# The modulation silu(c) @ ada_w in a hybrid decoder layer: float32 products on 32-column strips of TensorE in place of multiply-adds on VectorE

## The chip, the core and the metric

The kernel runs on one core of a Trainium2 chip. The core's engines each work through a queue of their own, in order: TensorE (PE: matrix products, and the loads of their weights), VectorE (DVE), ScalarE (ACT), GpSimd (POOL), and SyncE (SP), whose queue issues nearly all of the DMAs. SBUF is the working memory, PSUM the eight banks into which PE writes. The metric is the device time of one execution in microseconds, lower is better.

## What is computed

One decoder layer on x (1024 tokens x 1024 features, float32) with a conditioning vector c of 1024 numbers. Cut to what matters here:

```
mod = silu(c) @ ada_w + ada_b                  # ada_w: 1024 x 6144
sh1, sc1, g1, sh2, sc2, g2 = split(mod, 6)     # 1024 numbers each
h  = rmsnorm(x, norm1_g) * (1 + sc1) + sh1
q, k, v, u = split(h @ w_in, 4)                # 512 columns each
o  = [rmsnorm(stick_breaking(q, k, v)), rmsnorm(s5(u))]
x  = x + g1 * (o @ w_out)
h  = rmsnorm(x, norm2_g) * (1 + sc2) + sh2
val, gate = split(causal_dwconv(h @ ffn_w_up), 2)
x  = x + g2 * ((gelu(gate) * val) @ ffn_w_down)
```

The change concerns the first line alone: a vector times a matrix of 24 MB, all in float32.

## The kernel before

Big products are made of float32r parts: an operand is split into hi and lo, and hi*hi + hi*lo + lo*hi are accumulated in PSUM, three products of 128x512 each. Smaller ones are plain float32. The program is written in the order of the work; a scheduler then sets the order of the instructions on each engine's queue, and tile pools with a fixed number of buffers (`bufs`) decide how early a load or a product may begin.

**Stage 1 (about 11 to 103 us): modulation of norm1, h, and the columns u.** For each feature block k = 0..7, 1 MB of ada_w (`ada_raw`, three buffers) holds 8 row blocks r of 128 rows, with 128 shift and 128 scale columns. For k = 0 PE makes the products directly, with the weights as the stationary operand and one column of c moving (L210, sixteen products of 128x1). For k = 1..7 DVE multiplies and adds: one TENSOR_SCALAR (L213) and seven SCALAR_TENSOR_TENSOR (through the helper `stt`, L67) on 128x256 into `ada_acc`; then two PE products with a column of ones (L218) sum over the 128 partitions. DVE adds bias and gain (S1c, A1); ACT applies them to the transposed x (L233) and splits off hi, POOL makes lo, and PE accumulates u (`u_mm`, L190 to L192). On DVE's queue this work is mixed with the parameters of the state-space part (`st`, `ek`, `Q`).

**Stage 2 (about 103 to 344 us): q, k, v and the state-space groups.** PE makes 24 token tiles of 24 products (`qkvp`, L551 to L553); in between stand four batches of the state-space part, whose products (`w1p`, `kp`, `vps`, `yps`, `gps`, float32) alternate with DVE's scans. `ada_back` (six calls of 512 columns: two for g1, two for sh2, two for sc2) is spread over the token tiles, three steps ahead of each: a step loads one row block (`ada_raw`, 256 KB) and DVE adds it into `ada_acc` (L67, 128x512). After eight steps PE sums over the partitions (`adps`, L571 or L575). Loads and `ada_acc` share the three buffers of the tag `uF`. PSUM: `psA` has four buffers of the tag `aux`, three of `mm`, one of `qt`.

**Attention (344 to 610 us)** and the output projections are not touched. **The MLP (640 to 1365 us)** is 22 pairs of up-projection tiles (`upps`, L916 to L918) and down-projections (`dnps`). `g2_rows` stands after the first pair: 16 row blocks of ada_w are added by DVE (L968, L67) into `g2acc`, and PE sums over the partitions (L972).

Of the kernel before, what the change touches and what calls it, by code (L numbers as in the profile page):

```python
# [20 lines left out]
D = 1024  # L21
# [14 lines left out]
def hybrid_layer_kernel(  # L36
# [23 lines left out]
    def tt(eng, out, a, b, op):  # L60
        eng.tensor_tensor(out=out, in0=a, in1=b, op=op)  # L61
# [9 lines left out]
    def rsqrt(pl, dst, v, n):  # L71
        """dst = 1 / sqrt(v), [128, n], to float32's accuracy."""
# [13 lines left out]
    # packed small parameters, one column (or row, on each partition) after the other  # L86
# [3 lines left out]
    cols2_sb = const.tile([128, 194], F32, name="cols2_sb")  # L90
# [3 lines left out]
    gq_sb, gk_sb = cols2_sb[:, 192:193], cols2_sb[:, 193:194]  # L94

# [9 lines left out]
    # added to the scores of the block on the diagonal: -1e30 where key >= query  # L105
# [7 lines left out]

    u_d = dram.tile([512, 8, 128], F32, name="u_d")
# [5 lines left out]
    # modulation: per-feature scale and shift columns, per-feature gate rows  # L120
# [6 lines left out]
    # ================= phase A: norm1, input projection, state space groups =================  # L127
# [35 lines left out]
    # per-token scale of norm1  # L163
# [35 lines left out]
    for k in range(NK):  # L199
# [5 lines left out]
        # shift and scale of 128 features  # L205
        mps = psU.tile([128, 512], F32, tag="mps", name="mps", bufs=1)
        if k == 0:
            for i in range(2):
                for r in range(8):
                    pe.matmul(mps[:, i:i + 1], lhsT=raw[:, r, i * 128:(i + 1) * 128], rhs=c_sb[:, r:r + 1], start=(r == 0), stop=(r == 7))  # L210
        else:
            acc = pn.tile([128, 256], F32, tag="ada_acc", name="ada_acc1")
            dve.tensor_scalar(out=acc, in0=raw[:, 0, :], scalar1=c_sb[:, 0:1], scalar2=None, op0=MUL)  # L213
            for r in range(1, 8):
                stt(acc, raw[:, r, :], c_sb[:, r:r + 1], acc, MUL, ADD)
            for i in range(2):
                cs_ = slice(i * 128, (i + 1) * 128)
                pe.matmul(mps[:, i:i + 1], lhsT=acc[:, cs_], rhs=ones[:, 0:1], start=True, stop=True)  # L218
        tt(dve, S1c[:, k:k + 1], mps[:, 0:1], sh1b[:, k:k + 1], ADD)
        stt(A1[:, k:k + 1], mps[:, 1:2], sc1b[:, k:k + 1], n1g_sb[:, k:k + 1], ADD, MUL)  # L220
# [90 lines left out]
    # powers a^1..a^8: pw[:, ri, k, pair]  # L311
# [22 lines left out]
    def cmul(eng, ore, oim, are, aim, bre_, bim_, tmp, conj=False):  # L334
        """(ore + i oim) = (are + i aim) * (bre + i bim), or * conj(b)"""
# [30 lines left out]
    # conj(e^{i 8 theta})^(2^k), k = 0..6  # L366
# [6 lines left out]
    # b * (e^{dt a} - 1) / a, in place  # L373
# [12 lines left out]
    # e^{-i 8 theta c} for c = 0..15, and for c = 0, 16, .. 112  # L386
# [9 lines left out]
    # coefficients of a pair of groups side by side, each on the partitions of its own states  # L396
# [6 lines left out]
    # delta(p div 16, j)  # L403
    blkid = sm.tile([128, 8], F32, name="blkid")
    dve.tensor_reduce(out=blkid, in_=ident.rearrange("p (j h) -> p j h", h=16), op=ADD, axis=AX.X)
    # delta(p mod 16, h)
# [13 lines left out]
    psA = alloc("psA", bufs=4, space=PSUM)  # L420
# [6 lines left out]
    def ssm_batch(ft):  # L427
        q0 = ft * 4
        qs = slice(q0, q0 + 4)
        # rotation table e^{-i 8 theta c}  # L430
# [3 lines left out]
        # Q[(par, p), pair, i, h] = a^{7-i} b  # L434
# [10 lines left out]
        # coefficients of the state's real and imaginary part in Re(C a^{j+1} s)  # L445
# [7 lines left out]
        # inputs of the groups: partition = (step in chunk, channel), free = chunk  # L453
# [4 lines left out]
        # transposed Q for the products with the inputs  # L458
# [5 lines left out]
        # impulse response inside a chunk, block lower triangular  # L464
# [17 lines left out]
        # chunk sums, rotated, then scanned over the chunks  # L482
# [46 lines left out]
        for j in range(8):  # L529
            sp.dma_start(out=ov[j], in_=gt[j * 16:(j + 1) * 16])  # L530

# [1 line left out]
    def load_wchunk(cix):  # L533
        his, los = [], []
        for k in range(NK):
# [554 lines left out]
```

## Time and profile before

| | us |
|---|---|
| median of three runs | 1371.71 (1368.38 to 1372.44) |
| the profiled execution: span from its first to its last instruction | 1365.3 |
| PE busy | 1261.6 (92%) |
| DVE busy | 953.0 (70%) |
| ACT busy, POOL busy | 375.6 (28%), 385.3 (28%) |
| mean granted TensorE clock, as a share of full speed | 0.959 |

The profile is of one execution, whose own time is known by its span; what lies around the span is not in the profile. Busy time of PE is modelled for the ends of its products, so that products in a row overlap: their rate is read from the distance of their starts. TensorE's clock has two levels, 2.4 GHz (1.00 in the profile's column) and 1.2 GHz; a value between them is a mean over a stretch.

### The profile page before, as it was taken

The page shows a single profiled execution, that of the slowest core. Times are in us where ns is not written, and L with a number is a line of the kernel's source. Part 1 is how long each engine was busy: PE and PEld are TensorE (multiplying, and loading weights), DVE is VectorE, ACT ScalarE, POOL GpSimd, SP SyncE. Part 2 cuts the span into 40 slices and gives each one's busy share as a digit, 9 for nine tenths or more (in the row PEclk, how much of TensorE's full clock was granted, in tenths as well). Part 3 has the DMA queues.
Part 4 walks back from the last instruction along what each step waited for, and adds up shares of the span by engine and source line. Part 5 has one row for each costly group of instructions (what it writes and reads, how often), then busy time and mean ns, then how long its engine had stood idle before and what let it go on. Part 6 is the DMA issues. An engine that isn't in the chain of part 4 may idle for free.

```text
span 1365.3 us, 16015 instructions
## 1 busy us (share of the span) xinstructions
PE 1261.6 (92%) x5988; PEld 1034.5 (76%) x5988; DVE 953.0 (70%) x1465; ACT 375.6 (28%) x651; POOL 385.3 (28%) x369
## 2 busy tenths in 40 slices
PE   5979899898778996898999999999999999999998
PEld 4767778677557785676788888888888888888886
DVE  6999999873998889875775555455465655555555
ACT  5431233431765666444111101010101010101010
POOL 3562461530684449512130101111111111111100
PEclk9889889999889998898999999999999999999999
DMA  8452445657934663000620102020211111111103
GB/s 342 149 139 63 122 142 141 157 169 230 242 97 145 213 187 106 32 16 20 199 91 31 62 31 78 16 77 18 75 42 56 46 57 47 47 47 47 47 1 123
DMA packets 98264, 134.78 MB, mean 99 GB/s; under 512 B 33414, under 2 KB 66310, under 8 KB 97164
## 3 DMA queue, kind: packets, MB, share of 16 engines
q1 hardware_dynamic: 81292, 125.38, 29.5%
q10 hardware_dynamic: 16896, 8.39, 2.2%
q8 instruction: 47, 0.77, 0.2%
q14 instruction: 29, 0.24, 0.1%
HBM read 107.40 MB, written 25.17 MB: 97 GB/s over the span
## 4 chain that ended last, share of the span: by engine, by line
PE 64%; DVE 20%; DMA 7%; issue 3%; POOL 2%; ACT 2%; SPq 1%; DVEq 0%; ACTq 0%; POOLq 0%
PE upps L916 11%; PE upps L917 11%; PE upps L918 11%; PE dnps L1004 6%; PE dnps L1005 6%; PE dnps L1003 6%; DVE ada_acc L67 3%; DMA ada_raw<-in_ada_r_dram 3%; DVE nb L700 2%; PE wops L773 2%; PE wops L774 1%; PE wops L775 1%; POOL sig L61 1%; DVE st L61 1%; DMA x<-in_x_dram 1%
## 5 line engine op out<-in xcount | busy, mean ns | idle before, releaser
L916 PE MATMUL upps<-h2hi,uphi 128*128 128x512 f32 x704 | 275.5, 391 | 2.3 <-DVE cv L67 2.0
L917 PE MATMUL upps<-h2lo,uphi 128*128 128x512 f32 x704 | 274.6, 390 | 0.2 <-DVE h2lo L61 0.2
L918 PE MATMUL upps<-h2hi,uplo 128*128 128x512 f32 x704 | 274.4, 390 | 0.0
L953 ACT ACTIVATE cv<-upps,cols_sb 128x1024 f32<-128x1024 f32 x44 | 53.2, 1209 | 500.3 <-PE upps L918 500.3
L916 PEld LDWEIGHTS upps<-h2hi,uphi 128*128 128x128 f32 x704 | 132.4, 188 | 30.8 <-issue 2.8
L917 PEld LDWEIGHTS upps<-h2lo,uphi 128*128 128x128 f32 x704 | 132.4, 188 | 28.1 <-DVE h2lo L61 0.5
L918 PEld LDWEIGHTS upps<-h2hi,uplo 128*128 128x128 f32 x704 | 132.4, 188 | 27.6 <-issue 0.2
L61 DVE TENSOR_TENSOR uplo<-upraw,uphi 128x1024 fp32r<-128x1024 f32 x44 | 55.5, 1262 | 127.1 <-POOL uphi L161 127.1
L1004 PE MATMUL dnps<-wdlo,ahi 128*128 128x512 f32 x352 | 137.0, 389 | 0.9 <-DVE wdlo L61 0.9
L1003 PE MATMUL dnps<-wdhi,ahi 128*128 128x512 f32 x352 | 136.6, 389 | 0.6 <-POOL wdhi L161 0.6
L1005 PE MATMUL dnps<-wdhi,alo 128*128 128x512 f32 x352 | 136.9, 389 | 0.0
L161 POOL TENSOR_SCALAR uphi<-upraw 128x1024 fp32r<-128x1024 f32 x44 | 47.5, 1080 | 281.1 <-PE upps L917 200.0
L61 DVE TENSOR_TENSOR xs<-dnps,xs 128x512 f32<-128x512 f32 x88 | 60.9, 692 | 86.9 <-PE dnps L1005 86.9
L67 DVE SCALAR_TENSOR_TENSOR cv<-upps,cols_sb,cv 128x1023 f32<-128x1023 f32 x88 | 112.4, 1278 | 11.6 <-ACT cv L953 10.9
L61 POOL TENSOR_TENSOR sig<-sig,nb 128x127 f32<-128x127 f32 (+3 forms) x64 | 98.2, 1542 | 70.5 <-DVE nb L700 47.4
L700 DVE TENSOR_TENSOR_SCAN nb<-nb 128x128 f32<-128x128 f32 (+3 forms) x64 | 105.8, 1667 | 8.0 <-ACT nb L698 7.6
L67 DVE SCALAR_TENSOR_TENSOR ada_acc<-ada_raw,c_sb,ada_acc 128x256 f32<-128x256 f32 (+1 forms) x97 | 74.2, 779 | 24.5 <-DMA ada_raw<-in_ada_r_dram 21.2
L551 PE MATMUL qkvp<-w_hi,hhi 128*128 128x512 f32 x192 | 78.5, 410 | 3.4 <-DVE qssq L604 2.9
L552 PE MATMUL qkvp<-w_lo,hhi 128*128 128x512 f32 x192 | 78.5, 409 | 0.6 <-POOL w_lo L61 0.6
L553 PE MATMUL qkvp<-w_hi,hlo 128*128 128x512 f32 x192 | 78.0, 406 | 0.0
L1004 PEld LDWEIGHTS dnps<-wdlo,ahi 128*128 128x128 f32 x352 | 66.1, 188 | 15.0 <-DVE wdlo L61 1.3
L1003 PEld LDWEIGHTS dnps<-wdhi,ahi 128*128 128x128 f32 x352 | 65.9, 188 | 14.7 <-POOL wdhi L161 1.0
(240 smaller groups left out, 2370.7 us busy)
## 6 DMA issues: line engine op xcount, KB each, us to landing
upraw<-in_w_up_dram SPq DMA_DIRECT2D x44, 512.0 KB, 3.2
ada_raw<-in_ada_r_dram SPq DMA_DIRECT2D x48, 256.0 KB, 2.8
wdraw<-in_w_down_dram SPq DMA_DIRECT2D x22, 512.0 KB, 3.8
ada_raw<-in_ada_a_dram SPq DMA_DIRECT2D x8, 1024.0 KB, 9.3
qk_d<-hl ACTq DMA_DIRECT2D x32, 256.0 KB, 2.8
q<-qk_d SPq DMA_DIRECT2D x32, 256.0 KB, 5.7
w_raw<-in_w_qkv_dram SPq DMA_DIRECT2D x24, 256.0 KB, 3.9
xt<-in_x_dram SPq DMA_DIRECT2D x8, 512.0 KB, 5.5
```

The source lines that it names most:

```text
L61: eng.tensor_tensor(out=out, in0=a, in1=b, op=op)
L67: dve.scalar_tensor_tensor(out=out, in0=a, scalar=s, in1=b, op0=op0, op1=op1)
L551: pe.matmul(o, lhsT=lh, rhs=his[k], start=(k == 0), stop=False)
L552: pe.matmul(o, lhsT=lh, rhs=los[k], start=False, stop=False)
L553: pe.matmul(o, lhsT=ll, rhs=his[k], start=False, stop=(k == NK - 1))
L700: dve.tensor_tensor_scan(out=nb[:, 0:n][:, ::-1], data0=nb[:, 0:n][:, ::-1], data1=nb[:, 0:n][:, ::-1], initial=1.0, op0=MUL, op1=ALU.bypass)
L916: pe.matmul(o, lhsT=hi[:, k, :], rhs=rh, start=(k == 0), stop=False)
L917: pe.matmul(o, lhsT=hi[:, k, :], rhs=rl, start=False, stop=False)
L918: pe.matmul(o, lhsT=lo[:, k, :], rhs=rh, start=False, stop=(k == NK - 1))
L1003: pe.matmul(o, lhsT=hi[:, a], rhs=whi[:, b], start=(i == 0), stop=False)
L1004: pe.matmul(o, lhsT=hi[:, a], rhs=wlo[:, b], start=False, stop=False)
L1005: pe.matmul(o, lhsT=lo[:, a], rhs=whi[:, b], start=False, stop=(i == len(ops) - 1))
```

## The change

The vector silu(c) becomes the stationary operand. `c32` holds each row block's 128 values 32 times side by side, so that a product with `c32[:, r, :]` occupies 32 columns of the array and writes 32 equal rows of PSUM; row blocks r and r + 4 accumulate in strip r % 4, and the four strips fill the 128 partitions of one PSUM tile. That tile is copied to SBUF, and a product with a matrix of 1/32 (`mean32`) sums over the partitions. In stage 1 this serves all eight feature blocks, k = 0 too. In stage 2 the PSUM tile has a tag of its own (`ada`, one buffer), for which `aux` goes from four buffers to three; the accumulator in `uF` is needed only after the eighth row block. The biases of sh2 and sc2 come in `cols2` (16 more columns); that of g1 is loaded on all partitions.

```diff
-    cols2_sb = const.tile([128, 194], F32, name="cols2_sb")
+    cols2_sb = const.tile([128, 210], F32, name="cols2_sb")
...
+    sh2b, sc2b = cols2_sb[:, 194:202], cols2_sb[:, 202:210]
...
+    c32 = const.tile([128, 8, 32], F32, name="c32")
+    dve.tensor_copy(c32, c_sb.unsqueeze(2).to_broadcast([128, 8, 32]))
+
+    mean32 = const.tile([128, 128], F32, name="mean32")
+    pool.memset(mean32, 1.0 / 32.0)
+
+    def strips(ps, raws):
+        for r in range(8):
+            j = r % 4
+            pe.matmul(ps[32 * j:32 * j + 32], lhsT=c32[:, r, :], rhs=raws[r], start=(r < 4), stop=(r >= 4))
...
         mps = psU.tile([128, 512], F32, tag="mps", name="mps", bufs=1)
-        if k == 0:
-            for i in range(2):
-                for r in range(8):
-                    pe.matmul(mps[:, i:i + 1], lhsT=raw[:, r, i * 128:(i + 1) * 128], rhs=c_sb[:, r:r + 1], start=(r == 0), stop=(r == 7))
-        else:
-            acc = pn.tile([128, 256], F32, tag="ada_acc", name="ada_acc1")
-            dve.tensor_scalar(out=acc, in0=raw[:, 0, :], scalar1=c_sb[:, 0:1], scalar2=None, op0=MUL)
-            for r in range(1, 8):
-                stt(acc, raw[:, r, :], c_sb[:, r:r + 1], acc, MUL, ADD)
-            for i in range(2):
-                cs_ = slice(i * 128, (i + 1) * 128)
-                pe.matmul(mps[:, i:i + 1], lhsT=acc[:, cs_], rhs=ones[:, 0:1], start=True, stop=True)
-        tt(dve, S1c[:, k:k + 1], mps[:, 0:1], sh1b[:, k:k + 1], ADD)
-        stt(A1[:, k:k + 1], mps[:, 1:2], sc1b[:, k:k + 1], n1g_sb[:, k:k + 1], ADD, MUL)
+        strips(mps[:, 0:256], [raw[:, r, :] for r in range(8)])
+        acc = pn.tile([128, 256], F32, tag="ada_acc", name="ada_acc1")
+        dve.tensor_copy(acc, mps[:, 0:256])
+        for i in range(2):
+            pe.matmul(mps[:, 256 + i:257 + i], lhsT=acc[:, i * 128:(i + 1) * 128], rhs=mean32[:, 0:1], start=True, stop=True)
+        tt(dve, S1c[:, k:k + 1], mps[:, 256:257], sh1b[:, k:k + 1], ADD)
+        stt(A1[:, k:k + 1], mps[:, 257:258], sc1b[:, k:k + 1], n1g_sb[:, k:k + 1], ADD, MUL)
...
-    psA = alloc("psA", bufs=4, space=PSUM)
+    psA = alloc("psA", bufs=3, space=PSUM)
...
     def ada_back(ix):
         kind, o = divmod(ix * 512, 1024)
-        acc = wp.tile([128, 512], F32, tag="uF", name="ada_acc", bufs=3)
-        pool.memset(acc, 0.0)
-        sp.dma_start(out=acc[0:1, :], in_=ada_br[ix:ix + 1, :])
+        ps = psA.tile([128, 512], F32, tag="ada", name="adps", bufs=1)
+        if kind == 0:
+            sp.dma_start(out=g1row[:, o:o + 512], in_=ada_br[ix:ix + 1, :].to_broadcast([128, 512]))
         for r in range(8):
             raw = wp.tile([128, 512], F32, tag="uF", name="ada_raw", bufs=3)
             sp.dma_start(out=raw, in_=ada_r[ix, :, r])
-            stt(acc, raw, c_sb[:, r:r + 1], acc, MUL, ADD)
+            j = r % 4
+            pe.matmul(ps[32 * j:32 * j + 32], lhsT=c32[:, r, :], rhs=raw, start=(r < 4), stop=(r >= 4))
             yield
-        ps = psA.tile([128, 512], F32, tag="aux", name="adps")
+        acc = wp.tile([128, 512], F32, tag="uF", name="ada_acc", bufs=3)
+        act.activation(out=acc, in_=ps, func=AF.Copy)
         if kind == 0:
-            pe.matmul(ps, lhsT=ones, rhs=acc, start=True, stop=True)
-            act.activation(out=g1row[:, o:o + 512], in_=ps, func=AF.Copy)
+            pe.matmul(ps, lhsT=mean32, rhs=acc, start=True, stop=True)
+            tt(dve, g1row[:, o:o + 512], ps, g1row[:, o:o + 512], ADD)
         else:
             for j in range(4):
-                pe.matmul(ps[:, j:j + 1], lhsT=acc[:, j * 128:(j + 1) * 128], rhs=ones[:, 0:1], start=True, stop=True)
+                pe.matmul(ps[:, j:j + 1], lhsT=acc[:, j * 128:(j + 1) * 128], rhs=mean32[:, 0:1], start=True, stop=True)
...
     def g2_rows():
         for ix in range(6, 8):
...
+            ps = psD.tile([128, 512], F32, tag="dn", name="adps2", bufs=4)
+            for r in range(0, 8, 2):
+                raw = wq.tile([128, 2, 512], F32, tag="wdraw", name="g2raw", bufs=2)
+                sp.dma_start(out=raw, in_=ada_r[ix, :, r:r + 2])
+                for i in range(2):
+                    j = (r + i) % 4
+                    pe.matmul(ps[32 * j:32 * j + 32], lhsT=c32[:, r + i, :], rhs=raw[:, i, :], start=(r < 4), stop=(r >= 4))
             acc = wq.tile([128, 512], F32, tag="wdhi", name="g2acc", bufs=2)
-            for r in range(8):
-                if r % 2 == 0:
-                    raw = wq.tile([128, 2, 512], F32, tag="wdraw", name="g2raw", bufs=2)
-                    sp.dma_start(out=raw, in_=ada_r[ix, :, r:r + 2])
-                if r == 0:
-                    dve.tensor_scalar(out=acc, in0=raw[:, 0, :], scalar1=c_sb[:, 0:1], scalar2=None, op0=MUL)
-                else:
-                    stt(acc, raw[:, r % 2, :], c_sb[:, r:r + 1], acc, MUL, ADD)
-            ps = psD.tile([128, 512], F32, tag="dn", name="adps2", bufs=4)
-            pe.matmul(ps, lhsT=ones, rhs=acc, start=True, stop=True)
+            act.activation(out=acc, in_=ps, func=AF.Copy)
+            pe.matmul(ps, lhsT=mean32, rhs=acc, start=True, stop=True)
             tt(dve, g2row[:, sl], ps, g2row[:, sl], ADD)
```

Where the work now stands on the queues, at three places (a row is line, operation, output<-moving operand, weights, shape, and a count of like products in a row; the lines of the changed kernel are some 13 to 15 higher in stage 1, and 6 to 9 higher later on).

Stage 1, before, DVE's queue: the sums of two feature blocks (ada_acc_268 for k = 1, ada_acc_322 for k = 2) among the splits of w_u (wu_lo) and k = 1's shift and gain.

```order
L67 SCALAR_TENSOR_TENSOR ada_acc_268<-ada_raw_262,c_sb,ada_acc_268 128x256
L67 SCALAR_TENSOR_TENSOR ada_acc_322<-ada_raw_317,c_sb,ada_acc_322 128x256
L61 TENSOR_TENSOR wu_lo<-wu_raw,wu_hi 128x512 x2
L67 SCALAR_TENSOR_TENSOR ada_acc_322<-ada_raw_317,c_sb,ada_acc_322 128x256
L61 TENSOR_TENSOR S1c<-mps,cols_sb 128x1
L67 SCALAR_TENSOR_TENSOR A_89<-mps,cols_sb 128x1
```

Stage 1, now, PE's queue for k = 2: eight strip products in a row, transposes of x (tp) behind them, then the two products that sum the copied tile.

```order
L125 MATMUL mps<-ada_raw_318,c_84 32x256 x8
L237 MATMUL tp<-ident,xt_133 128x128
L237 MATMUL tp<-ident,xt_134 128x128
L237 MATMUL tp<-ident,xt_135 128x128
L237 MATMUL tp<-ident,xt_136 128x128
L237 MATMUL tp<-ident,xt_129 128x128
L237 MATMUL tp<-ident,xt_130 128x128
L237 MATMUL tp<-ident,xt_131 128x128
L237 MATMUL tp<-ident,xt_132 128x128
L224 MATMUL mps<-mean_86,ada_acc_331 128x1 x2
```

The eight sums of a block moved from DVE to PE, where they stand together; every block of stage 1 does so but one, of whose eight strips the first and the last stand alone.

Stage 2, before, DVE's queue: single multiply-adds of ada_back between the state-space part (dtm, S, T) and the norm of q (qssq, rs_i).

```order
L67 SCALAR_TENSOR_TENSOR ada_acc<-ada_raw,c_sb,ada_acc 128x512
L61 TENSOR_TENSOR dtm_1168<-R_1176,T_1077 128x4x127
L64 TENSOR_SCALAR qssq<-qssq 128x16
L67 SCALAR_TENSOR_TENSOR ada_acc<-ada_raw,c_sb,ada_acc 128x512
L61 TENSOR_TENSOR S_1185<-dtm_1167,dtm_1168 128x4x127
L75 TENSOR_SCALAR rs_i<-qssq 128x16
L67 SCALAR_TENSOR_TENSOR ada_acc<-ada_raw,c_sb,ada_acc 128x512
```

Stage 2, now, PE's queue in the first call of ada_back: strip products (adps) between the products of one token tile.

```order
L557 MATMUL qkvp<-w_hi,hhi_103 128x512
L574 MATMUL adps<-ada_raw,c_84 32x512
L558 MATMUL qkvp<-w_lo,hhi_103 128x512
L574 MATMUL adps<-ada_raw,c_84 32x512
L559 MATMUL qkvp<-w_hi,hlo_111 128x512
```

The 48 row blocks stand on PE's queue as 22 single strips, 10 pairs and 2 triples, 34 groups in all, with other products between them; the last is 96 qkvp products ahead of the end of the v tiles.

The MLP, now, PE's queue: g2's first four strips behind the 96th product of the up-projection, the last of the second tile (h2hi_5842); before, the 97th product followed the 96th with nothing between.

```order
L925 MATMUL upps<-h2hi_5842,uphi 128x512
L926 MATMUL upps<-h2lo_5850,uphi 128x512
L927 MATMUL upps<-h2hi_5842,uplo 128x512
L977 MATMUL adps_6342<-g2raw,c_84 32x512 x4
L925 MATMUL upps<-h2hi_5843,uphi 128x512
```

Six pairs of strips follow, each among later upps.

## Rows read from the trace of the kernel before

**Rows 1.** The page's first part: the span, then for two engines the busy time, its share of the span and the number of instructions.

```profile
span 1365.3 us, 16015 instructions
...
PE 1261.6 (92%) x5988; PEld 1034.5 (76%) x5988; DVE 953.0 (70%) x1465; ACT 375.6 (28%) x651; POOL 385.3 (28%) x369
```

**Rows 2.** Stretches of the span, microseconds from its start. The columns: the stretch and its length, busy time (and instructions) of PE, of PE's weight loads, of DVE, ACT and POOL, the granted clock of TensorE as a share of full speed, the DMA share, GB/s.

```profile
11.00:90.30 79.30, 71.88 (x316) 58.25 (x316) 75.40 (x236) 39.21 (x65) 46.19 (x34) 0.91 0.58 201
90.30:103.40 13.10, 5.48 (x26) 4.90 (x25) 12.69 (x57) 3.91 (x7) 3.61 (x4) 0.59 0.66 164
103.40:344.00 240.60, 221.09 (x1153) 178.15 (x1153) 200.85 (x360) 68.75 (x116) 83.41 (x75) 0.92 0.53 149
640.00:690.00 50.00, 47.79 (x204) 38.19 (x203) 34.82 (x38) 9.83 (x11) 11.88 (x10) 0.98 0.47 149
700.00:1365.00 665.00, 659.50 (x2908) 545.12 (x2906) 360.00 (x373) 68.38 (x59) 80.79 (x77) 1.00 0.15 50
```

**Rows 3.** What PE waited for from the start to 345 us: the waiting group, what released it, the total in us, how often, the longest.

```profile
PE w1p L462 <- DVE Q L61: 6.3, 1, 6.3
PE qkT L613 <- DVE hl L67: 3.9, 1, 3.9
PE mps L218 <- DVE ada_acc L67: 3.9, 3, 1.6
PE adps L575 <- issue: 3.6, 1, 3.6
PE qkvp L551 <- DVE qssq L604: 2.9, 1, 2.9
PE yps L513 <- DVE rs_i L75: 2.3, 1, 2.3
PE yps L514 <- DVE S L61: 2.2, 1, 2.2
...
PE qkT L613 <- DVE hl L61: 1.6, 1, 1.6
...
PE w1p L462 <- DVE ek L61: 1.3, 1, 1.3
```

**Rows 4.** The groups of DVE's instructions that accumulate the modulation, over the whole span: line, operation, tiles and shapes, count | busy us, mean ns of one | idle time just before them and what ended it.

```profile
L67 DVE SCALAR_TENSOR_TENSOR ada_acc<-ada_raw,c_sb,ada_acc 128x512 f32<-128x512 f32 x48 | 45.2, 942 | 24.5 <-DMA ada_raw<-in_ada_r_dram 21.2 <-DMA ada_acc<-in_ada_br_dram 3.3
...
L67 DVE SCALAR_TENSOR_TENSOR ada_acc<-ada_raw,c_sb,ada_acc 128x256 f32<-128x256 f32 x49 | 29.0, 620 | 0.0
...
L67 DVE SCALAR_TENSOR_TENSOR g2acc<-g2raw,c_sb,g2acc 128x512 f32<-128x512 f32 x14 | 10.9, 778 | 2.4 <-DMA g2raw<-in_ada_r_dram 2.2
...
L213 DVE TENSOR_SCALAR ada_acc<-ada_raw,c_sb 128x256 f32<-128x256 f32 x7 | 3.6, 519 | 0.0
...
L968 DVE TENSOR_SCALAR g2acc<-g2raw,c_sb 128x512 f32<-128x512 f32 x2 | 1.0, 518 | 6.5 <-DMA g2raw<-in_ada_r_dram 6.5
```

**Rows 5.** PE's instructions in order of time at three places of the state-space work: start us, us, line, output<-moving, weights, the part of the array as rows*columns, the shape of the moving operand, records. A float32 product leaves two records, so x12 is six products.

```profile
142.37 0.49 PE L513 MATMUL yps<-S,W 64*128 64x128 f32 x2
142.70 0.38 PE L514 MATMUL yps<-S,W 64*128 64x128 f32 x2
143.01 0.49 PE L512 MATMUL yps<-U,W 128*128 128x128 f32 x2
143.43 0.48 PE L513 MATMUL yps<-S,W 64*128 64x128 f32 x2
...
148.87 1.50 PE L522 MATMUL gps<-ys,G 128*128 128x128 f32 x12
150.21 0.60 PE L462 MATMUL w1p<-ident,Q 128*128 128x128 f32 x4
...
213.35 1.97 PE L488 MATMUL vps<-U,W 128*64 128x128 f32 x32
215.25 0.66 PE L613 MATMUL qkT<-ident,qk 128*128 128x128 f32 x4
```

**Rows 6.** The same view where g2 is reduced over the partitions: a float32 product of 128x512 (adps) among the float32r products of the MLP (upps, one record each).

```profile
666.76 1.02 PE L972 MATMUL adps<-g2acc,ones 128*128 128x512 f32 x2
667.22 0.79 PE L916 MATMUL upps<-h2hi,uphi 128*128 128x512 f32 x1
667.85 0.39 PE L917 MATMUL upps<-h2lo,uphi 128*128 128x512 f32 x1
668.08 0.40 PE L918 MATMUL upps<-h2hi,uplo 128*128 128x512 f32 x1
```

**Rows 7.** The same view, the first product of the third up-projection tile; in brackets the idle time before it and what ended it.

```profile
660.53 0.47 PE L916 MATMUL upps<-h2hi,uphi 128*128 128x512 f32 x1 [1.97 <-DVE cv L67]
```

**Rows 8.** The same view: the sixteen products of 128x1 that make the first feature block's shift and scale, and, for a later block, the two that sum over the partitions (four records) with what follows them.

```profile
11.02 6.96 PE L210 MATMUL mps<-c_sb,ada_raw 128*128 128x1 f32 x32 [11.02 <-DVE inv L67]
...
42.59 0.50 PE L218 MATMUL mps<-ones,ada_acc 128*128 128x1 f32 x4
42.95 1.40 PE L190 MATMUL ups<-hhi,wu_hi 128*128 128x512 f32 x5
```

**Rows 9.** The tiles ada_raw (the loaded pieces of ada_w): who sat idle until such a load had landed (us, times), and the time of a load from issue to landing.

```profile
  DMA ada_raw<-in_ada_r_dram: 21.2, 16
...
DMA to landing us min/median/max: 2.6/2.8/11.8
```

More of the change, by code (lines that the diff above doesn't have):

```diff
@@ L566, in ada_back @@
             sp.dma_start(out=raw, in_=ada_r[ix, :, r])
-            stt(acc, raw, c_sb[:, r:r + 1], acc, MUL, ADD)
+            j = r % 4
+            pe.matmul(ps[32 * j:32 * j + 32], lhsT=c32[:, r, :], rhs=raw, start=(r < 4), stop=(r >= 4))
             yield
-        ps = psA.tile([128, 512], F32, tag="aux", name="adps")
+        acc = wp.tile([128, 512], F32, tag="uF", name="ada_acc", bufs=3)
+        act.activation(out=acc, in_=ps, func=AF.Copy)
         if kind == 0:
-            pe.matmul(ps, lhsT=ones, rhs=acc, start=True, stop=True)
-            act.activation(out=g1row[:, o:o + 512], in_=ps, func=AF.Copy)
+            pe.matmul(ps, lhsT=mean32, rhs=acc, start=True, stop=True)
+            tt(dve, g1row[:, o:o + 512], ps, g1row[:, o:o + 512], ADD)
         else:
             for j in range(4):
-                pe.matmul(ps[:, j:j + 1], lhsT=acc[:, j * 128:(j + 1) * 128], rhs=ones[:, 0:1], start=True, stop=True)
+                pe.matmul(ps[:, j:j + 1], lhsT=acc[:, j * 128:(j + 1) * 128], rhs=mean32[:, 0:1], start=True, stop=True)
             ks = slice(o // 128, o // 128 + 4)
             if kind == 1:
-                act.activation(out=S2c[:, ks], in_=ps[:, 0:4], func=AF.Copy)
+                tt(dve, S2c[:, ks], ps[:, 0:4], sh2b[:, ks], ADD)
             else:
-                stt(A2[:, ks], ps[:, 0:4], 1.0, n2g_sb[:, ks], ADD, MUL)
+                tt(dve, A2[:, ks], ps[:, 0:4], sc2b[:, ks], ADD)
+                stt(A2[:, ks], A2[:, ks], 1.0, n2g_sb[:, ks], ADD, MUL)
         yield
@@ L1044, in layouts @@
                                  col(a["ffn_conv_w"][0]), col(a["ffn_conv_b"][0]),
-                                 twice(a["q_norm_g"][0]), twice(a["k_norm_g"][0])], axis=1)
+                                 twice(a["q_norm_g"][0]), twice(a["k_norm_g"][0]),
+                                 col(adb[3]), col(adb[4])], axis=1)
     r["ada_a"] = ada[:, :, 0:2].reshape(8, 128, 2, 8, 128).transpose(3, 1, 0, 2, 4).reshape(8, 128, 8, 256)
```

## The prediction

> **What bounds the kernel now.** I read first the page's busy times, then the span cut into stretches, then what PE waits for, and last PE's instructions in order of time. PE is busy for 92% of the span and DVE for 70% [rows 1], but that is a mean over stages. In the MLP after 700 us PE is busy for 659.5 of 665.0 us at full clock [rows 2]: there PE alone sets the time, and whatever is added to its queue is paid in full. In stage 1 (11 to 103.4 us) DVE is busy for 88.1 of 92.4 us; PE stands idle for 92.4 - 77.4 = 15.0 us [rows 2], of which 6.3 + 1.3 + 3.9 = 11.5 us end on DVE [rows 3]. There DVE leads. In stage 2 (103.4 to 344 us) both are full: PE 221.1 and DVE 200.9 of 240.6 us [rows 2].
>
> Stage 2 decides. All of PE's present work there stays, so the stage can become shorter only by time that PE now loses. PE waits for 240.6 - 221.1 = 19.5 us; of these 3.9 + 2.9 + 2.3 + 2.2 + 1.6 = 12.9 us end on DVE, and 3.6 us stand before the last sum of the modulation [rows 3]: 16.5 us that the change can reach. The granted clock is 0.92 [rows 2], a mean of the levels 2.4 and 1.2 GHz; (1 - 0.92) x 240.6 = 19.2 us are lost to the lower one. In the same way stage 1 loses 0.09 x 79.3 = 7.1 us and, of its last 13.1 us, 0.41 of the 5.5 busy ones, 2.2 us: 9.3 us. So PE has 15.0 + 9.3 + 19.5 + 19.2 = 63.0 us of lost time in the two stages. The question is whether the new products fit in.
>
> **What goes.** DVE loses 45.2 + 29.0 + 10.9 + 3.6 + 1.0 = 89.7 us of multiply-adds [rows 4] and gains eight copies and the copy that makes c32, each of a size with the 0.5 us of the 128x256 operation at L213 [rows 4]. PE loses the sixteen products for k = 0, 6.96 us, and gains two sums for k = 0, 42.95 - 42.59 = 0.36 us [rows 8]. ACT's six copies in stage 2 hide, since ACT is busy for 68.8 of 240.6 us, and so do two broadcast loads of g1's bias, 0.5 MB at a DMA share of 0.58 [rows 2]; without that cover each load would delay a block of ada_w by about the 2.8 us that 256 KB take to land [rows 9].
>
> **The price of a strip product.** A float32 product of 128x512 holds PE for 667.85 - 666.76 - 0.23 = 0.86 us, where 0.23 us (668.08 - 667.85) is the float32r product behind it [rows 6]; 256 columns take half, 0.43 us. No row shows four strips. The nearest is vps: sixteen 128x128 products that alternate between two 64-column halves of the array take 215.25 - 213.35 = 1.90 us, 0.119 each; with the whole array gps takes (150.21 - 148.87) / 6 = 0.223 us [rows 5]. So two strips do run side by side. Bounds for a group of strips: one after the other (0.86 us each), or up to four at once (0.86 us for all). I take two at once, as the row shows.
>
> By the Trainium skill (TensorE: Matmul & The Clock Gate, section Part 3: Packing small matmuls) products in different column groups of the array run concurrently, starting about 4 ns apart. vps agrees for two; nothing here shows four. By that rule the four strips cost what one does, which is the rival "four at once" below.
>
> Entering and leaving the narrow mode costs too. vps takes 0.12 us more than sixteen halves of 0.223, and shows only the leaving; yps, where products on 64 rows and on the whole array alternate, takes 143.43 - 142.37 = 1.06 us for three products instead of 0.67, 0.39 us more [rows 5]. Bounds 0.12 and 0.39 us a group; I take 0.24, vps twice.
>
> **What PE gains.** Stage 1: eight groups of eight strips, 8 x (4 x 0.43 + 0.24) = 15.6 us; with -6.96 + 0.36 that is +9.0 us. Stage 2: in the new order the 48 strips stand as 22 singles, 10 pairs and 2 triples among qkvp products. A single costs as much as a pair: (22 + 10) x 0.86 + 2 x 1.71 + 34 x 0.24 = 39.1 us. That is the point of this change: a row block loaded alone gets no neighbour to share the array with. g2: one group of four and six pairs, 1.71 + 6 x 0.86 + 7 x 0.24 = 8.6 us. The first group stands just where PE waits 1.97 us for a cv of DVE's [rows 7], and hides there: +6.6 us, paid in full. Sum: +54.7 us.
>
> **What comes back.** Stage 1: the 11.5 us of waits on DVE go, since PE now leads and `ada_acc` no longer stands ahead of `Q`. Stage 2: three quarters of the 16.5 us, 12.4; a quarter stays because the chain through qk, qssq, qinv and qkT is a latency that DVE's free time shortens but doesn't remove. The lower clock: two thirds of 9.3 and of 19.2, 6.2 + 12.8 us; if waits alone caused it, it would go with them, but between the ends (nothing, all) I keep a third for stretches of small products. Against it stands a new wait. DVE waited 21.2 us in 16 places for `ada_raw` to land, 2.8 us from issue [rows 9]; the wait now stands on PE's queue, with the qkvp and state-space products behind it, for which DVE and ACT wait in turn. There are three buffers instead of two and other work between groups, so I take a fifth, 4.2 us (bounds 0 and 21.2). Back: 11.5 + 6.2 + 12.4 + 12.8 - 4.2 = 38.7 us.
>
> One buffer fewer of `aux` I put at nothing: only the two vps tiles must live together, and adps leaves the tag. The sums over the partitions, which now wait for ACT's copy, stand behind other products in the new order. If that fails, w1p and kp of the next batch are late, with the 2 us waits of yps [rows 3] as the size, four times.
>
> **Sum.** 54.7 - 38.7 = +16.0 us: stage 1 about -8.7, stage 2 about +18.1, g2 +6.6. On the profiled execution that is 1365.3 + 16.0 = 1381.3 us of span; the median of the runs is 6.4 us above that span, so 1371.7 + 16.0 = 1387.7, say **1388 us**. Attention is untouched and starts later by what stages 1 and 2 add up to.
>
> **Rivals.**
> *Faster: the strips fill time that PE loses anyway.* One mechanism in stages 1 and 2: with DVE relieved, PE never waits, its clock stays at the upper level, and all 63.0 us come back: 54.7 - 63.0 = -8.3, 1363 us. It decides from 87% recovered on (54.7 / 63.0); my forecast is 61%. For it: DVE's chain is what most of the waits end on. Against: latencies, and loads on PE's queue.
> *Four at once.* Stage 1 +2.2, stage 2 34 x (0.86 + 0.24) = 37.4, g2 7 x 1.10 - 1.97 = 5.7: 45.3 - 38.7 = +6.6, 1378 us. It changes little because singles fill stage 2.
> *The change doesn't do what it says: strips run one after the other.* In-order issue, or whatever else keeps neighbours apart, would do it. Stage 1 +22.7, stage 2 41.3 + 8.2 = 49.5, g2 +13.5: 85.7 - 38.7 = +47.0, 1419 us. Against it stands vps.
> *Loads stall PE.* All 21.2 us move from DVE to PE: +17.0 on the forecast, 1405 us.
>
> **Chances and range.** Forecast 0.40, four at once 0.20, filled time 0.17, stalled PE 0.11, one after the other 0.12. The range 1362 to 1415 leaves out most of the last and the lower half of the filled time. About 0.3% (4 us) is what a measurement of this kernel can tell from no change: faster 0.20, same 0.10 (the edges of "filled time" and "four at once"), slower 0.70.
>
> **What the profile would show.** Right: qkvp starts before 100 us; a single strip among qkvp pushes the next start out by about 1.1 us, a group of eight of 256 columns takes about 2 us; stage 2 ends later though DVE is busy for some 45 us less in it; PE waits little; g2 adds 5 to 9 us between the 96th and the 212th upps. Wrong: a group of eight under 1.2 us or over 3 us; PE's waits on `ada_raw` above 10 us; a clock in stage 2 of 0.98 or more, with the waits gone; or the attention's start unmoved.

## The result, and the profile after

The changed kernel takes 1383.67 us (median of 4 runs, 1382.77 to 1385.71), the kernel before in the same comparison 1371.26 us: ratio 1.0103, interval [1.0075, 1.0131], 12 us slower by the medians and 14 by the ratio. The time lies within 5 us of the 1388 us forecast. Several terms of the sum do not, and what made the kernel slow is not quite what the sum says.

The page's first lines of the changed kernel, as [rows 1]:

```profile
span 1383.8 us, 16360 instructions
...
PE 1294.5 (94%) x6216; PEld 1021.6 (74%) x6216; DVE 857.1 (62%) x1360; ACT 380.1 (27%) x655; POOL 362.2 (26%) x364
```

DVE lost 95.9 us of work and PE gained 32.9. The span profiled of the kernel before lies some 6 us under its median, that of the changed kernel lies at its median, so the two spans differ by 18.5 us and the medians by 12.4; differences between stages below come from the traces and add up to the larger figure.

Stretches of the changed kernel, with the columns of [rows 2]:

```profile
11.00:96.00 85.00, 75.35 (x441) 55.86 (x441) 67.88 (x268) 43.82 (x72) 43.45 (x35) 0.96 0.55 198
96.00:140.00 44.00, 35.60 (x160) 20.88 (x160) 23.90 (x49) 4.39 (x7) 11.86 (x13) 0.92 0.42 109
140.00:300.00 160.00, 160.00 (x874) 114.24 (x873) 96.81 (x221) 53.63 (x83) 53.85 (x46) 1.00 0.53 145
...
96.00:344.69 248.69, 239.66 (x1230) 169.11 (x1230) 131.16 (x287) 66.81 (x104) 72.12 (x69) 0.99 0.53 148
700.00:1383.80 683.80, 677.93 (x2978) 558.37 (x2976) 376.27 (x384) 71.80 (x62) 89.31 (x82) 1.00 0.16 52
```

Stage 2 of the kernel before, from its first qkvp to the first product of the attention (`z`, made of k and q):

```profile
103.40:337.94 234.54, 216.07 (x1134) 174.62 (x1134) 196.56 (x353) 64.31 (x102) 80.72 (x72) 0.93 0.52 145
```

Stage 1 ends at 96.0 us instead of 103.4 (first qkvp). Stage 2 is measured from there to the first z, because both kernels have done the same work by then: the 1230 - 1134 = 96 records more are those of the 48 strips. It ends at 344.7 us instead of 337.9 and is 14.1 us longer. From 140 to 300 us PE is never idle and its granted clock is 1.00: what the rival "filled time" described did come true there. The first 44 us of the stage are another matter. PE's waits up to 350 us, as [rows 3]:

```profile
PE mps L125 <- DMA ada_raw<-in_ada_a_dram: 11.2, 1, 11.2
PE adps L574 <- DMA ada_raw<-in_ada_r_dram: 8.4, 1, 8.4
PE mps L224 <- DVE ada_acc L222: 3.7, 2, 3.4
PE ups L203 <- ACT hhi L171: 2.4, 1, 2.4
```

The first is the start of the program, as in [rows 8]. Of stage 2's many waits on DVE one of 0.6 us is left, ahead of the first z; one wait on a load has come, 8.4 us in one place. PE and SP's queue there, in order of time (for SP: start us, us to issue, line, what is moved, count):

```profile
97.83 1.70 PE L494 MATMUL vps<-U,W 128*64 128x128 f32 x28
107.93 1.91 PE L574 MATMUL adps<-ada_raw,c 128*32 128x512 f32 x2 [8.40 <-DMA ada_raw<-in_ada_r_dram]
```

```profile
96.91 1.59 SPq L544 DMA_DIRECT2D w_raw<-in_w_qkv_dram  x2
99.00 2.56 SPq L210 DMA_DIRECT2D u_d<-uF  x3
101.66 0.99 SPq L544 DMA_DIRECT2D w_raw<-in_w_qkv_dram  x1
102.73 0.93 SPq L572 DMA_DIRECT2D ada_raw<-in_ada_r_dram  x1
```

The strip was next in PE's queue at 99.5 us, and its block of ada_w was not even issued before 102.73, behind the last copies of u. Those copies read the three uF buffers, and `ada_raw` uses the same three. But the shared buffers are not all of it. ScalarE's last copy of u into them:

```profile
93.99 0.59 ACT L209 ACTIVATE uF<-ups 128x512 f32<-128x512 f32 x1
```

u was ready at 94.58 us, and SP issued its copies from 99.00 on only: they stand behind loads of `w_raw`, for which SP had waited 6.8 us on a `w_lo` of POOL's.

The price of strips (float32 products of 32 columns), PE in order of time: a group of eight of 256 columns, a single of 512 among qkvp, a group of four and a pair in g2.

```profile
26.65 1.07 PE L125 MATMUL mps<-ada_raw,c 128*32 128x256 f32 x16 [0.25 <-PE tp L237]
27.66 1.09 PE L237 MATMUL tp<-ident,xt 128*128 128x128 f32 x8
...
113.46 0.39 PE L557 MATMUL qkvp<-w_hi,hhi 128*128 128x512 f32 x1
113.78 1.04 PE L574 MATMUL adps<-ada_raw,c 128*32 128x512 f32 x2
114.76 0.50 PE L558 MATMUL qkvp<-w_lo,hhi 128*128 128x512 f32 x1
115.09 0.39 PE L559 MATMUL qkvp<-w_hi,hlo 128*128 128x512 f32 x1
...
668.72 1.06 PE L977 MATMUL adps<-g2raw,c 128*32 128x512 f32 x8
669.72 0.50 PE L925 MATMUL upps<-h2hi,uphi 128*128 128x512 f32 x1
...
676.97 1.05 PE L977 MATMUL adps<-g2raw,c 128*32 128x512 f32 x4
677.96 0.50 PE L926 MATMUL upps<-h2lo,uphi 128*128 128x512 f32 x1
```

Four strips take 669.72 - 668.72 = 1.00 us, a pair 0.99, a single 114.76 - 113.78 = 0.98: four run side by side. Around a single the float32r steps, 0.23 us elsewhere [rows 6], are 0.32 ahead of it and 0.33 behind it, so a group of one to four costs 0.98 + 0.09 + 0.10 = 1.17 us at full clock, however many strips it holds. (By the Trainium skill, TensorE: Matmul & The Clock Gate, section Part 3: Packing small matmuls, products in different column groups run concurrently; the g2 rows agree for four.)

### The profile page after: what moved, and what is told of

The parts are those of the page before. It is cut to its first block, busy times and chain, and to the rows that moved or that the text cites. A ratio compares the mean times of both kernels' runs of the same rounds, so it can differ in the third digit from the quotient of the medians.

```text
span 1383.8 us, 16360 instructions
## 1 busy us (share of the span) xinstructions
PE 1294.5 (94%) x6216; PEld 1021.6 (74%) x6216; DVE 857.1 (62%) x1360; ACT 380.1 (27%) x655; POOL 362.2 (26%) x364
## 4 chain that ended last, share of the span: by engine, by line
PE 81%; DVE 11%; DMA 3%; issue 3%; ACT 1%; POOL 1%; SPq 0%; DVEq 0%; POOLq 0%; ACTq 0%
PE upps L925 12%; PE upps L926 12%; PE upps L927 12%; PE dnps L1012 6%; PE dnps L1013 6%; PE dnps L1011 6%; DVE nb L709 4%; PE qkvp L558 3%; PE qkvp L557 3%; PE qkvp L559 3%; PE adps L574 2%; DVE wl L61 2%; PE wops L782 1%; PE wops L784 1%; PE wops L783 1%
## 5 line engine op out<-in xcount | busy, mean ns | idle before, releaser
L61 POOL TENSOR_TENSOR sig<-sig,nb 128x127 f32<-128x127 f32 (+3 forms) x64 | 93.2, 1465 | 73.8 <-DVE nb L709 44.6
L709 DVE TENSOR_TENSOR_SCAN nb<-nb 128x128 f32<-128x128 f32 (+3 forms) x64 | 109.6, 1725 | 2.9 <-ACT nb L707 2.7
L1013 PEld LDWEIGHTS dnps<-wdhi,alo 128*128 128x128 f32 x352 | 66.1, 188 | 13.8
```

The costliest lines, as they stand in the source:

```text
L709: dve.tensor_tensor_scan(out=nb[:, 0:n][:, ::-1], data0=nb[:, 0:n][:, ::-1], data1=nb[:, 0:n][:, ::-1], initial=1.0, op0=MUL, op1=ALU.bypass)
L1013: pe.matmul(o, lhsT=lo[:, a], rhs=whi[:, b], start=False, stop=(i == len(ops) - 1))
```

## The experiments

All ratios are to the kernel before, run beside each kernel on the same chip; a difference in us behind a ratio is worked out from it. Two marks in the traces serve below: the first z, and the oT, VectorE's 32 pieces of the attention's result.

**One part alone: three kernels.** Each is the kernel before with one of the three edits: `strips()` in stage 1; `ada_back` on strips (with its adps bank, so aux at three); `g2_rows` on strips.

> Only stage 1's modulation goes to strips; the back half (g1, sh2, sc2) and g2 stay on VectorE as before, and aux keeps its four buffers. My theory (each part costs what its own products show in TensorE's queue): stage 1 ends about 7 us sooner, as in the changed kernel (first qkvp at 96.0 instead of 103.4 us), and this is kept to the end: ratio 0.995, about 1364 us. Rival (stage 2 is bound by VectorE, so what stage 1 saves is waited away there): the first qkvp comes 7 us sooner, stage 2 ends less than 2 us sooner, ratio 0.998 to 1.000.

Measured: 1359.62 us, ratio 0.9943 [0.9921, 0.9965], -7.8 us. The size is the theory's, and the rival is out. The place is not shown; the first line is of this kernel, the second of the kernel before:

```profile
L557 PE MATMUL qkvp<-w_hi,hhi x192: 387/389/1414, 102.6 to 325.3; 128*128 128x512 f32 x192
L551 PE MATMUL qkvp<-w_hi,hhi x192: 387/389/793, 103.4 to 331.8; 128*128 128x512 f32 x192
```

The first qkvp starts only 0.8 us sooner, with no products ahead of it but those of the kernel before and the strips; the last one starts 6.5 us sooner. So in this trace most of the gain arises behind stage 1. The execution profiled is the slowest of eight, 6 us over their median, and where a median one gains is not on record.

> Only the back half's modulation (g1, sh2, sc2) goes to strips, with aux at three buffers as in the changed kernel; stage 1 and g2 stay on VectorE. My theory: this part carries most of the loss: 34 interruptions of about 1.17 us are 39.8 us, against some 12 us of VectorE waits and up to 19 us of the lower clock that come back, plus one stall of about 8 us on the first load: +8 to +14 us, ratio 1.006 to 1.010. Rival (as forecast, with a third of the clock loss kept and waits on loads spread over the stage): +18 us, ratio 1.013. Second question: the attention stretch of the changed kernel was 5 us longer; if the back half's new order in the program does that, it shows here too, with the last product of the attention 5 us later than stage 2's end explains; if not, it is a difference between two executions.

Measured: 1381.01 us, ratio 1.0090 [1.0068, 1.0112], +12.3 us: the theory's range, but not by the theory's pieces. The strips of this kernel stand in 29 groups, not 34 (33.9 us), and its first load does not stall PE, which waits for loads in two other places:

```profile
PE adps L581 <- DMA ada_raw<-in_ada_r_dram: 4.8, 2, 3.1
```

On the second question: the attention's first oT is 5.7 us late in this trace and its last 8.9, so 3.2 us are added on the way. In g2_only, whose products stand in the attention as before, the same two marks are 1.5 and 4.2 us early, a drift of 2.7 us the other way with nothing changed there. The 3 us are no more than that; and from the first z, which is 12.8 us late, the lag falls.

> Only g2's modulation goes to strips; stage 1 and the back half stay on VectorE. The forecast's term: +6.6 us, ratio 1.005. By the group price that the changed kernel's trace shows (1.0 us and 0.2 us around it, seven groups, less the 2 us wait that goes): +6.4 us, which is no different. Rival (the MLP stretch was 8.9 us longer in the changed kernel because of this part alone): +9 us, ratio 1.0065. Second rival (the MLP has slack after all): within 1 us of before.

Measured: 1376.03 us, ratio 1.0055 [1.0033, 1.0077], +7.5 us. The forecast's term and the rival both lie in the interval; "slack in the MLP" is out. The trace splits it. From the 96th to the 212th upps, where the strips stand, it takes 36.1 us instead of 30.4, 5.7 more; another 2.5 us come behind them, where no product was changed. So it is in the changed kernel; PE in the middle of the MLP, in the kernel before and in the changed one:

```profile
1000.00:1300.00 300.00, 300.00 (x1325) 248.43 (x1324) 162.20 (x167) 31.31 (x27) 37.79 (x36) 1.00 0.14 48
1000.00:1300.00 300.00, 300.00 (x1320) 247.57 (x1320) 160.93 (x168) 30.13 (x26) 37.69 (x36) 1.00 0.14 45
```

PE is full and at full clock in both, and gets through 0.4% fewer of the same products; from the 212th upps to the end it takes 679.3 us instead of 676.8. All kernels built from the changed one lose 2.4 to 3.8 us there, s1_only and ab_only too, where g2 stands as before; of the kernels before with one edit, those of the runs aux3 and before_own below, none loses more than 0.4. The cause is open.

The parts add up to -7.8 + 12.3 + 7.5 = +12.0 us, ratio 1.009, inside the changed kernel's interval. That is weaker than it looks: each interval reaches about 3 us to either side, the 2.5 us stand in all three parts, and the back half alone has other groups and other waits than in the changed kernel.

**The lost aux buffer, in the kernel before.**

```
-    psA = alloc("psA", bufs=4, space=PSUM)
+    psA = alloc("psA", bufs=3, space=PSUM)
```

> The kernel before with one change: aux, the PSUM buffers of the state-space batches, three instead of four. The forecast costed this at nothing: ratio 0.999 to 1.001. Rival: the products of the next batch wait for a buffer, four times 2 us or more: ratio 1.005 and waits before w1p, kp, vps or yps that the kernel before does not have.

Measured: 1378.92 us, ratio 1.0082 [1.0056, 1.0109], +11 us: far from nothing. It did not show as waits of w1p or vps. PE, in this kernel and then in the kernel before, at the last sum of the modulation, behind which the first products of the attention stand:

```profile
344.52 1.83 PE L575 MATMUL adps<-ones,ada_acc 128*128 128x1 f32 x8 [10.74 <-issue]
346.21 0.45 PE L694 MATMUL z<-k,q 128*128 128x128 f32 x1
```

```profile
336.66 1.42 PE L575 MATMUL adps<-ones,ada_acc 128*128 128x1 f32 x6
337.94 0.45 PE L694 MATMUL z<-k,q 128*128 128x128 f32 x1
```

With three buffers the state-space batches run late: the last gps (a batch ends with these) starts at 307.7 us instead of 295.3. VectorE's multiply-adds wait longer for their blocks of ada_w; its waits from 255 to 400 us:

```profile
DVE ada_acc L67 <- DMA ada_raw<-in_ada_r_dram: 24.8, 11, 4.2
```

(15.9 us in the kernel before). PE stands 10.74 us, 3.6 before [rows 3], ahead of the last sums. The profile names no releaser for that wait, but VectorE's rows do; its last multiply-add of the modulation, in this kernel and in the kernel before:

```profile
343.66 0.75 DVE L67 SCALAR_TENSOR_TENSOR ada_acc<-ada_raw,c_sb,ada_acc 128x512 f32<-128x512 f32 x1
335.39 0.75 DVE L67 SCALAR_TENSOR_TENSOR ada_acc<-ada_raw,c_sb,ada_acc 128x512 f32<-128x512 f32 x1 [1.91 <-DMA ada_raw<-in_ada_r_dram]
```

It ends 0.1 us before the sums start, in both. That wait hangs on work of VectorE that the changed kernel no longer has. It is not the whole loss, though: the first z is 8.3 us late, the first oT only 0.8, the third 14.4 and the last 12.2, and the attention's products stand in another order than before. What carries the 11 us through the attention is not shown, and whether they can be carried over to the changed kernel is open.

**The stall: u's copies out of uF.** The changed kernel with

```
-        uF = wp.tile([128, 8, 64], F32, tag="uF", name="uF", bufs=3)
+        uF = pn.tile([128, 8, 256], F32, tag="ada_raw", name="uF", bufs=3)[:, 0:2, :].rearrange(...)
```

> The changed kernel with one edit: the copies of u on their way to memory use stage 1's freed ada_raw buffers instead of uF, so that the first three blocks of ada_w for stage 2 can be loaded during stage 1. In the changed kernel TensorE stood still for 8.4 us on the first of these blocks. My theory: that stall goes and nothing takes its place: 8 us less than the changed kernel, about 1375 us, ratio to before 1.003. Rival (the products behind the stall would have waited for the state-space chain anyway): less than 2 us, ratio 1.009.

Measured: 1366.31 us, ratio 0.9974 [0.9962, 0.9987]: 17 us less than the changed kernel, twice what I expected, and faster than the kernel before. Stretches of this kernel:

```profile
96.00:140.00 44.00, 44.00 (x227) 31.75 (x226) 38.76 (x71) 8.53 (x15) 14.24 (x14) 1.00 0.49 131
140.00:300.00 160.00, 159.53 (x888) 115.42 (x889) 115.32 (x220) 56.18 (x85) 61.01 (x51) 1.00 0.54 150
```

PE is full at full clock from 96 us to the last qkvp, where the changed kernel had lost 8.4 us to the stall and, standing still, fell to the lower clock level for some time (mean 0.92, 0.08 x 44.0 = 3.5 us). The order differs too: the 48 strips now stand in 27 groups instead of 34, since blocks that are loaded earlier arrive together. Seven groups at 1.17 us are 8.2. Together that is 20.1 us, but it is an account by counts and prices; only the total was measured. Against it stands a new wait on a load at the end of the stage, ahead of the last two strips:

```profile
329.83 2.60 PE L574 MATMUL adps<-ada_raw,c 128*32 128x512 f32 x4 [3.40 <-DMA ada_raw<-in_ada_r_dram]
```

And the traces do not put all of the gain into stage 2: at the first z this kernel is 9.8 us ahead of the changed one, at the last oT 15.7. Some six of the 17 us come in the attention, whose products stand in yet another order.

> The kernel before with the one edit of the run own_buf: u's copies leave uF for stage 1's freed buffers, so that the first three blocks of ada_w for stage 2 can be loaded during stage 1. A control: is the 1.3% that this edit gave back a property of the strips (the wait stood in TensorE's queue, ahead of the projection), or of the buffers in either kernel? Theory: of the strips; in the kernel before the wait stood in VectorE's queue, and the edit gives under 4 us, ratio 0.997 to 1.000. Rival: of the buffers; about 15 us here too, ratio 0.989.

The control, the same edit in the kernel before: 1373.97 us, ratio 1.0039 [1.0017, 1.0061]. It loses a little there, where I expected a small gain. So the gain belongs to the kernel with strips. That the late load hurts because it stands in PE's queue, with qkvp behind it, is read from the row of 8.40 us; the control doesn't show it by itself, since its order changed too (PE waits for 27.9 us from the first qkvp to the first z, 18.5 before).

**Fours instead of singles.** On top of the last edit, one load of four blocks, and four strips when it has landed; the copied sum moves to another tag:

```
+            if r % 4 == 0:
+                raw = stg.tile([128, 4, 512], F32, tag="ada4", name="ada_raw", bufs=1)
+                sp.dma_start(out=raw, in_=ada_r[ix, :, r:r + 4])
+            if r % 4 == 3:
+                for j in range(4):
+                    pe.matmul(ps[32 * j:32 * j + 32], lhsT=c32[:, r - 3 + j, :], rhs=raw[:, j, :], ...)
...
-        acc = wp.tile([128, 512], F32, tag="uF", name="ada_acc", bufs=3)
+        acc = wp.tile([128, 512], F32, tag="wraw", name="ada_acc", bufs=4)
```

> The changed kernel with the back half's strips in fours: one load of four blocks of ada_w into an 8 KB buffer instead of four loads, so that four strips become ready together; u's copies leave uF as in the run before, and aux stays at three buffers. Same 48 strips, same sums, 15 groups instead of 34. My theory (what costs is the group, 1.0 us and 0.2 us around it, however many strips it holds): 15 x 1.2 = 18 us instead of 34 x 1.17 = 40 us, and no first stall: 22 to 30 us less than the changed kernel, 1354 to 1362 us, ratio to before 0.988 to 0.994. Rival (strips cost per strip, or stage 2 is then bound by a chain of VectorE and ScalarE work): under 12 us less, ratio above 1.000.

Measured: 1362.14 us, ratio 0.9944 [0.9922, 0.9966]. Against the changed kernel that is 21.5 us less, just under the range expected; against own_buf only 4.2, although twelve groups fewer are 14 us. The same stretches show where much of the rest went:

```profile
96.00:140.00 44.00, 43.30 (x245) 33.21 (x244) 41.11 (x77) 10.38 (x17) 14.75 (x15) 1.00 0.46 125
140.00:300.00 160.00, 152.97 (x888) 116.03 (x888) 105.82 (x212) 53.64 (x81) 62.42 (x50) 0.98 0.60 168
```

From 140 to 300 us PE waits for 7.0 us (0.5 in own_buf), among it 3.0 for a load, 1.9 for qk and 1.5 for vt, a part of v, and 0.02 x 160 = 3.2 us go to the lower clock. 14.0 - 6.6 - 3.2 = 4.2; that this meets the measured figure is luck, since the rows cover a part of the stage only, and at the first z this kernel is 6.2 us ahead of own_buf. The reading is that strips taken out of a full queue uncover the waits that they had filled.

> The grouped kernel with g2 back on VectorE's multiply-adds. Theory (in the MLP TensorE alone sets the time, so g2's seven groups are paid in full): 5.5 to 6.5 us less than the grouped kernel. With that, the fastest kernel of the study if the groups do what I expect: about 1350 us, ratio to before 0.985. Rival: the MLP's share is not g2's products but their place, and under 3 us come back.

Measured: 1358.83 us, ratio 0.9922 [0.9898, 0.9945], the fastest kernel of the study: 25 us below the changed kernel and 11 below the kernel before. Taking g2 back gives 3.3 us on the run group4, near the rival's bound; the two intervals overlap, so the 5.5 us expected are not excluded. The two traces speak for them: from the 96th to the 212th upps 29.6 us instead of 36.1, 6.5 less.

> The run before with one edit: each group of four is summed on its own, in an aux buffer that is held for some 3 us, so that adps gives its bank back and aux has four buffers again; six more sums over the partitions. Theory A (the lost buffer itself costs, as the 0.8% of the kernel before with three buffers suggested): 5 to 8 us less than the run before, w1p, kp and vps of the last batches earlier. Theory B (that loss came through the order in which the attention's products were put, which in the grouped kernel with three buffers is again that of the kernel before): no gain, within 3 us of the run before.

Measured: 1416.29 us, ratio 1.0331 [1.0305, 1.0356]: neither theory. The edit moved more than the buffer. SP's queue in this kernel, and in the run group4:

```profile
SPq L463 <- PE yps L518: 58.2, 3, 19.8
SPq L573 <- PE adps L577: 36.9, 9, 24.0
```

```profile
SPq L463 <- PE yps L518: 22.7, 3, 11.5
...
SPq L573 <- PE adps L576: 20.3, 6, 5.7
```

SP waits for PE much longer, in its one queue, ahead of the loads of U (L463) and of those of ada_w (L573); PE is idle for 34.6 of the 249 us from 96 on. What a fourth buffer is worth is not answered by this.

> The run own_buf (all strips as in the changed kernel, u's copies out of uF) with aux at two buffers instead of three. The kernel before lost 0.8% when aux went from four to three. Theory (with the strips VectorE is early, buffers come free sooner, and aux was rightly costed at nothing in the changed kernel): within 4 us of own_buf, ratio to before 0.995 to 1.000. Rival (buffers of aux cost as in the kernel before): 10 us or more over own_buf, ratio 1.005 or more.

Measured: 1386.50 us, ratio 1.0127 [1.0097, 1.0157], 20 us over own_buf. The rival's outcome, but again not by a wait that the trace puts down to a buffer: PE is idle for less than 1 us from 96 to 300 us. The strips stand in 36 groups instead of 27 (9 x 1.17 = 10.5 us) and the last gps starts at 319.7 us instead of 287.7. Buffers of aux do count with the strips in place; the step from four to three alone stays unmeasured there.

> Stage 1's modulation on strips, the back half and g2 on VectorE, aux at four buffers, and u's copies out of uF: what a kernel without the back half's strips reaches with the better buffers. Theory (with no stall the back half's strips fill lost time and are worth about nothing by themselves): within 4 us of the grouped kernel with g2 on VectorE, 1355 to 1363 us, ratio 0.990 to 0.995. Rival A (the back half belongs on TensorE): 1365 us or more. Rival B (it belongs on VectorE): 1352 us or less.

Measured: 1365.04 us, ratio 0.9968 [0.9946, 0.9991], 6 us over the grouped kernel with g2 on VectorE, and the two intervals just fail to touch: rival A, by a hair. But s1_only, the same kernel without the edit of uF, has 0.9943, and its interval overlaps with that of the grouped kernel (0.9922) as with this one's. So the best kernel with the back half on TensorE is 3 us faster than the best one without, which the intervals do not tell from nothing: that the back half, in fours, is worth moving isn't shown.

**Neighbours in the same strip.** In `strips()` of the changed kernel:

```
-            j = r % 4
-            pe.matmul(..., start=(r < 4), stop=(r >= 4))
+            j = r // 2
+            pe.matmul(..., start=(r % 2 == 0), stop=(r % 2 == 1))
```

> The changed kernel with stage 1's eight strips in the order of strips 0,0,1,1,2,2,3,3 instead of 0,1,2,3,0,1,2,3: the same eight products of 256 columns, but neighbours in the queue now often write the same strip. Theory (products side by side run at once only because they lie in different strips): a group takes 2 to 2.4 us instead of 1.0, stage 1 about 8 to 11 us longer, some of it under the waits on VectorE's copies. Rival (narrow products are simply faster, wherever they lie): 1.0 us a group and no difference.

Measured: 1385.39 us, ratio 1.0114 [1.0085, 1.0144], as the changed kernel. PE in order of time:

```profile
26.75 1.09 PE L125 MATMUL mps<-ada_raw,c 128*32 128x256 f32 x16 [0.25 <-PE tp L237]
27.78 1.09 PE L237 MATMUL tp<-ident,xt 128*128 128x128 f32 x8
...
39.32 0.62 PE L125 MATMUL mps<-ada_raw,c 128*32 128x256 f32 x2
39.87 0.50 PE L204 MATMUL ups<-hlo,wu_hi 128*128 128x512 f32 x1
```

A group of eight takes 27.78 - 26.75 = 1.03 us, not 2 to 2.4: my theory of neighbours falls. The rival's reason falls too, since a single narrow product of 256 columns takes 0.55 us and one of 512 takes 0.98, no less than four. What fits every row is that a group lasts as long as its fullest strip (two products of 0.43 us, or one of 0.86) and 0.12 to 0.17 us more, and that a second product on a strip does not hold back those behind it. How far that reaches was not tried.

## Why the prediction was right or wrong

**Direction and size: right**, +16.0 us forecast, +12 to +14 measured, in part by luck: the terms err in both directions, and two of the four signs that I had named for a wrong forecast came.

**Strips at two at once: wrong.** Four run at once; a group of eight takes 1.01 us and not 2, under the 1.2 that I named as a refutation. The vps row [rows 5] shows two halves of the array and could show no more than two. By the rival "four at once" this takes 9.4 us off the sum. Stage 1 pays 7 x 1.20 + 1.17 + 2 x 0.74 = 11.1 us instead of 15.6 (one of its blocks stands as a six, 0.98 us, and two singles, 0.55 us each, with 0.19 around each group); stage 2 is made of singles and pairs and loses little by it.

**Stage 2's price: right.** 34 groups at 1.17 us are 39.8 us, 39.1 forecast; the 1.10 for a single was 1.17.

**What comes back in stage 2: mis-sized on both sides.** PE's idle time went from 234.5 - 216.1 = 18.5 us to 248.7 - 239.7 = 9.0, of which 8.4 is the stall: 17.9 us back, not 12.4. The lower clock cost 0.07 x 234.5 = 16.4 us and now 0.01 x 248.7 = 2.5: 13.9 back, not 12.8. Against them the new wait on loads, 8.4 us in one place instead of 4.2 spread out. 39.8 - 17.9 - 13.9 + 8.4 = +16.4, 18.1 forecast; the stretch grew by 14.1 us. The account is good to some 3 us. A clock of 0.99 with the waits gone stood in my list of what would prove the forecast wrong, and it came: the mechanism of the rival "filled time" was at work. What kept the kernel slow were the groups, 34 of them, and a late first load; with the load early, own_buf ends on the other side, at 0.9974.

**What comes back in stage 1: too much.** I took all 11.5 us of DVE's waits. Idle time went from 15.0 to 9.65 us, 5.4 back: PE still waits for VectorE's copy (L222) and for ACT. The clock gave (9.3 - 0.04 x 85) = 5.9, forecast 6.2. With 11.1 - 6.96 + 0.36 = 4.5 paid: -6.8 us, against -7.4 in the trace and -8.7 forecast. Errors of 6 us in what comes back and of 4.5 in the price mostly cancel. That s1_only measures -7.8 is no proof of this, since its trace gains elsewhere.

**g2: right.** +6.6 forecast, +7.5 alone, of which the trace shows 5.7 where the strips stand; by the price of a group it is 7 x 1.17 - 1.97 = 6.2. The 2.5 us behind them stand in no term of the sum.

**aux four to three at nothing: not borne out.** In the kernel before it costs 11 us, from three to two 20 us in own_buf. In both the order of the products changed, and no wait is put down to such a buffer; that the order is the cause is not shown. For the changed kernel's own step no run tells.

**Attention untouched: only in what it computes.** Its products stand in another order in the changed kernel. From the first z to the last oT it takes 241.1 us, 238.5 before, and the lag grows from 6.8 to 9.3 us. But g2_only and group4, whose order there is that of the kernel before, take 235.5 and 235.1 us, and s1_only, with the same order too, 240.5. A difference of 2.6 us is within what comes with no change there, so this stays open.

## What to carry to other kernels

An operation moved to an in-order engine takes its load's wait with it, and everything queued behind pays (8.4 us here): look at which buffers its first load shares, and with what. On TensorE count groups of narrow products, not products: bring them together by loading together. And once an engine's queue is full, taking work out of it returns only what no wait then uncovers. A part tried alone gets an order of its own, too: the same 48 strips stood in 34, 29, 27 and 36 groups, so that prices carry over and sums of parts do so only roughly.

## What was not expected of the hardware

A group of narrow float32 products costs 0.98 to 1.00 us for one, two or four of 512 columns, and the order of strips inside a group of eight changes nothing (1.01 and 1.03 us). The same products of the MLP, with PE full at full clock, went through 0.4% slower in all kernels built from the changed one. And, though not of the hardware: an edit of one number of buffers moved the whole kernel by 11 to 20 us, with no wait in the trace put down to that buffer.
